# A two-layer PEER encoder: layer 0 also dense for 224 tokens in its V stage with a third sparse group, activations copied in pieces during U2, one-number gathers as steps of their own, x turned in 16 columns

## The chip, the cores and the metric

The kernel runs on one core of a Trainium2 chip. The metric is the device time of one execution in microseconds (us), the median over several runs. A profile is one execution that the hardware profiler recorded. Engines: PE is TensorE's matmul, PEld its weight load, DVE is VectorE, ACT is ScalarE, POOL is GpSimd, SP is SyncE, whose queue issues the plain loads.

## What is computed

A trunk of two layers for 256 tokens of width 1024, with 16 learned tokens put in front (272 tokens in layer 0, 256 in layer 1). Layer 0's mixer is a gated linear recurrence in both directions, layer 1's a conformer convolution. Each mixer is followed by PEER, which takes most of the time and all of the change:

```python
def peer_block(xc, w_query, sub_keys, expert_u, expert_v):
    ...
    s1, i1 = lax.top_k(scores[:, :, 0], PEER_TOPK)
    s2, i2 = lax.top_k(scores[:, :, 1], PEER_TOPK)
    cand = (s1[..., :, None] + s2[..., None, :]).reshape(c, PEER_HEADS, PEER_TOPK * PEER_TOPK)
    s, flat = lax.top_k(cand, PEER_TOPK)
    ...
    expert = idx1 * PEER_N_KEYS + idx2
    g = jax.nn.softmax(s.astype(jnp.float32), axis=-1).astype(xc.dtype)
    u = expert_u[expert]
    act = jax.nn.gelu(jnp.einsum('chkd,cd->chk', u, xc))
    v = expert_v[expert]
    return jnp.einsum('chk,chkd->cd', g * act, v)
```

Each token has 8 heads, each head picks 16 of 128 x 128 experts, and an expert is a row u and a row v of 1024 numbers.

## The kernel before

**Dense tokens.** Most tokens are computed against all 16,384 experts and the unpicked ones weighted with zero. Stage U loads the u rows as 128 pieces j of 128 rows (512 KB each). Each is split into a rounded part hi (ACT, L143) and a rest lo (DVE or POOL, L150), and 24 matmuls (L178) give the products of 128 experts with all dense tokens; ACT puts their gelu into `act_a` (j below 64, stage U1) or `act_b` (stage U2). In U2 the routing weights are made as products of one-hot matrices, 8 tokens to a unit (`g_unit`, L639 to L663), and multiplied into the activations of those tokens that are dense in V too. Stage V loads the v rows in the same way. For each j, eight matmuls of hi with the activations' two parts side by side (L701, twice as wide as the number of dense tokens) and eight of lo (L705, as wide as the number) add to eight accumulators that stay in PSUM. DVE makes the activations' second part for four j at a time (`w`, L262).

**Sparse groups.** The remaining tokens go in groups of 16; with 8 heads, a group fills the 128 partitions. A group of the early kind needs for each of its 16 picks one gathered u row per partition (L975, 512 KB a gather), a product with x (L984, "dot"), then one gathered v row (L975) and a multiply-add into `few_out` (L1024, "add"; the first is L1022). Ten of the early group's 16 dots run in U1 already. At the end eight pairs of matmuls (L740) put `few_out` on the accumulators. A late group does the same but picks its experts during V. A drawn group was dense in U: its picked activations already stand in `act_a` and `act_b`, so the whole activations of its 16 tokens are copied (POOL, L993), dumped as a table to DRAM (L995), and 16 gathers of one number per partition (L999, a "draw") fetch the picked ones; then come its v rows.

Which tokens are which is set by `DENSE_U`, `DENSE_V`, `EARLY`, `LATE` and `DRAWN` for (layer 0, layer 1). Before: layer 0 has 240 dense tokens, one early and one late group and no drawn one; layer 1 has 240 dense in U and 208 in V, one early and two drawn groups.

**Order.** `few_plan` lists the groups' steps one after the other, 70 in layer 0 and 72 in layer 1, and spreads them evenly over 111 of V's 128 j; `few_step`, called once per j, gives out what is due, one step of the pending picks (top-16 of scores on DVE: MAX, MAX_INDEX, MATCH_REPLACE, then softmax) included. The scheduler then orders every engine's queue, and each engine runs its queue strictly in that order. Row buffers: three, so a gather needs the add of three rows before. lo has two buffers, hi three, raw loads four. The x of a sparse group (`wide`) is made by matmuls of x with the unit matrix (`few_pick`), from copies of x's columns for the 8 heads that POOL writes (`xw`, L943), and is saved to DRAM and reloaded by `few_load` in V.

Of the kernel before, what the change touches and what calls it, by code (L numbers as in the profile page):

```python
# [31 lines left out]
CC = 8  # L32
HC = 8
FEW = META
DENSE_U, DENSE_V = (240, 240), (240, 208)
EARLY, LATE, DRAWN = ((256,), (240,)), ((240,), ()), ((), (224, 208))
DOTS_FROM, DOTS, AHEAD, LO_FROM = 48, 10, 2, 41
JG = 4
JA = 64
FULL = (("v", 1024),)  # L40
SQ_AT = 4
PE_TAPS = (0, 0, 0, 0, 0, 6, 31, 31)
# [18 lines left out]
class Trunk:  # L61
# [481 lines left out]
    def peer(self, layer, n, xs):  # L543
# [10 lines left out]
        with tc.tile_pool(name=f"few{layer}", bufs=1) as kp:  # L554
# [5 lines left out]
            with tc.tile_pool(name=f"top{layer}", bufs=1) as sp:  # L560
# [30 lines left out]
                drawn = [self.few_pick(sp, kp, q, xs, layer, t0) for t0 in DRAWN[layer]]  # L591

                def u_store(j, ps):
                    if j >= LO_FROM and len(picked[-1]) == 2:
                        with tc.issue_after(self.dve_lo.ins):
                            try:
                                next(slow)
                            except StopIteration as end:
                                picked[-1] += end.value
                    k, step = divmod(3 * (j - DOTS_FROM), 4)  # L600
                    if early and 0 <= k < DOTS + AHEAD and step < 3:
                        with tc.issue_after(self.dve_lo.ins), tc.issue_after(self.lo_ins.ins):
# [12 lines left out]
                    if 0 < t <= len(picked) and not odd:
                        with tc.issue_after(last.ins), tc.issue_after(self.mm.ins):
                            self.topk_out(*picked[t - 1], iT, ghT, glT)
                self.linears([U[j] for j in range(JA)], xs, nu, lambda j: FULL if j >= LO_FROM else (("p", 1024),), u_store)

            with tc.tile_pool(name=f"act1{layer}", bufs=1) as ap1:  # L620
                act_b = ap1.tile([P, NK - JA, nu], F32, name="act_b")
                hot_pool = tc.tile_pool(name=f"hot{layer}", bufs=2)
                hp = hot_pool.__enter__()

                def weigh(dst, g):
                    nc.vector.scalar_tensor_tensor(dst, g, scale, dst, op0=OP.mult, op1=OP.mult)  # L626
# [41 lines left out]
                def u_out(i, ps):  # L668
                    cd = at[0] * CC
                    w = act_b[:, i, :]  # L670
                    if cd < nu:
                        nc.scalar.activation(w[:, cd:], ps[:, cd:], AF.Gelu_apprx_tanh)
                    if cd > 0:
                        tmp = hp.tile([P, n], F32, tag="tmp", name="tmp")
                        nc.scalar.activation(tmp[:, :cd], ps[:, :cd], AF.Gelu_apprx_tanh)
                        nc.vector.tensor_tensor(w[:, :cd], w[:, :cd], tmp[:, :cd], op=OP.mult)  # L676
                    upto = min(len(chunks), (i + 1) * len(chunks) // (NK - JA - 4))
                    for c0 in chunks[at[0]:upto]:
                        g_unit(c0, JA + i + 1)
                    at[0] = upto  # L680

                acc = []
                self.upper(f"gate{layer}")
                self.linears([U[j] for j in range(JA, NK)], xs, nu, (("v", 1024),), u_out)
                hot_pool.__exit__(None, None, None)
                with tc.tile_pool(name=f"drawn{layer}", bufs=1) as sp:
                    for few in drawn:
                        self.few_dump(sp, few, act_a, act_b, layer)
                idx_pool.__exit__(None, None, None)
                self.upper(f"high{layer + 1}")  # L690
                row_pool = tc.tile_pool(name=f"rows{layer}", bufs=1)
# [228 lines left out]
    def few_pick(self, sp, kp, q, xs, layer, t0):  # L920
# [12 lines left out]
               "act": kp.tile([P, TOPK], F32, name=f"act{t0}"), "z": kp.tile([P, TOPK], F32, name=f"z{t0}")}  # L933
        if drawn:
            return few
        wide = sp.tile([P, D], F32, tag="kept" if early else "rows", name="wide", bufs=1 if early else AHEAD + 1)
        for h in range(2):
            pw = self.bank(5 + h, "wide_ps")
            for lo in range(2):
                xw = sp.tile([P, 4, HEADS, FEW], F32R, tag="xw", name="xw", bufs=2)  # L940
                for k in range(4):
                    src = xs(4 * h + k, lo).bitcast(F32)[:, None, t].to_broadcast([P, HEADS, FEW])
                    nc.gpsimd.tensor_copy(xw[:, k], src)  # L943
                for k in range(4):
                    nc.tensor.matmul(pw[:, k * P:(k + 1) * P], xw[:, k].rearrange("p h t -> p (h t)"), self.eye,
                                     start=k + lo == 0, stop=k + lo == 4, skip_group_check=True)
            nc.scalar.activation(wide[:, 512 * h:512 * h + 512], pw, AF.Copy)
        kept = self.dp.tile([P, D], F32, name=f"wide{layer}_{t0}")
        nc.sync.dma_start(kept, wide)
        return few | {"x": wide, "kept": kept}  # L950

    def few_topk(self, sp, few, layer):
        nc = self.nc
# [32 lines left out]
        if nxt < hi:  # L986
            few["rows"][nxt] = self.few_rows(pool, few, self.a["u_rows"], 0, nxt, ahead + 1)

    def few_dump(self, sp, few, act_a, act_b, layer):
        nc, t = self.nc, slice(few["t0"], few["t0"] + FEW)  # L990
        own = sp.tile([P, NK, FEW], F32, name=f"own{few['t0']}", bufs=1)
        for part, act in ((own[:, :JA], act_a), (own[:, JA:], act_b)):
            nc.gpsimd.tensor_copy(part, act[:, :, t])  # L993
        few["table"] = self.dp.tile([P, NK, FEW], F32, name=f"own{layer}_{few['t0']}")
        nc.gpsimd.dma_start(few["table"], own)  # L995

    def few_draw(self, few):
        for k in range(TOPK):
            self.nc.gpsimd.indirect_dma_start(  # L999
                out=few["act"][:, k:k + 1], out_offset=None, in_=few["table"].rearrange("p j (t o) -> (p j t) o", o=1),  # L1000
                in_offset=bass.IndirectOffsetOnAxis(ap=few["ids"][:, 0, k:k + 1], axis=0))

    def few_gelu(self, few, last):
        self.nc.scalar.activation(few["act"], few["act"], AF.Gelu_apprx_tanh)
        if last:
            self.warm(AF.Abs_reciprocal_sqrt)

    def few_load(self, vp, few):
        few["x"] = vp.tile([P, D], F32, tag="wide", name="wide", bufs=2)
        self.nc.sync.dma_start(few["x"], few["kept"])  # L1010

    def few_weigh(self, few, scale):
        self.nc.vector.scalar_tensor_tensor(few["act"], few["act"], scale, few["z"], op0=OP.mult, op1=OP.mult)
# [13 lines left out]

    def few_plan(self, vp, kp, early, late, drawn, scale, layer, ahead=2):
        steps = []
        for few in early + late + drawn:  # L1030
            lo = DOTS if few in early else 0
            if few["drawn"]:
                steps += [lambda few=few: self.few_draw(few)]
            else:
                steps += [lambda few=few: self.few_load(vp, few)]
                steps += [lambda few=few, lo=lo, k=k: self.few_dot(vp, few, k, lo, TOPK, ahead) for k in range(TOPK - lo + ahead)]
# [268 lines left out]
```

## Time and profile before

| | us |
|---|---|
| median of 3 runs | 1842.99 (1842.84 to 1844.76) |
| profiled execution | 1845.79 |
| its span | 1844.0 |
| layer 0: stage U1 / U2 / V, about | 176 to 345 / 345 to 556 / 556 to 890 |
| layer 1: mixer / U1 / U2 / V, about | 890 to 1051 / 1099 to 1272 / 1272 to 1472 / 1472 to 1816 |
| PE busy in the span | 1774.1 |

A row of a timeline gives start, duration, engine, line, operation and tiles (out<-in), and in brackets how long the engine had been idle before it and what ended that. A row of groups gives count, busy time, mean ns of one, idle time before. In windows the last three numbers are the granted TensorE clock (1.00 is full), the busy share of the 16 DMA engines, and GB/s.

### The profile page before, as it was taken

What the parts mean: (1) busy time and instruction counts of PE and PEld (TensorE: products, weight loads), DVE (VectorE), ACT (ScalarE), POOL (GpSimd) and SP (SyncE); (2) the same over time, 40 slices, a digit from 0 to 9 for tenths busy, and PEclk for the clock granted to TensorE, in tenths of its full rate; (3) what the DMA queues carried; (4) which work ended last, traced back from release to release, by engine and by line L of the source; (5) the groups of instructions that cost most, each with busy time, mean ns of one, the idle gap of its engine ahead of it and who ended that gap; (6) DMA issues with size and microseconds to landing.
All of it is one profiled execution on the core that took longest, in us unless ns stands there. A gap on an engine that the chain in (4) does not pass through costs nothing.

```text
span 1844.0 us, 35027 instructions
## 1 busy us (share of the span) xinstructions
PE 1774.1 (96%) x13500; PEld 1696.2 (92%) x13500; DVE 1513.8 (82%) x2863; ACT 916.2 (50%) x1510; POOL 486.1 (26%) x346
## 2 busy tenths in 40 slices
PE   8999999999999999999998999999999977999996
PEld 7899999999998999999887999999999967999996
DVE  7786996989999777786799869968889876868775
ACT  6544444454444545875432554445544534445552
POOL 1113993100002222130000129931000057423210
PEclk9999999999999999999999999999999988999998
DMA  5444567755558888887441445677555566889883
GB/s 195 160 161 145 185 196 247 247 169 164 162 173 305 289 306 278 294 318 238 161 140 35 140 154 185 196 250 246 171 171 171 173 251 226 311 304 341 293 293 126
DMA packets 111257, 395.17 MB, mean 214 GB/s; under 512 B 13169, under 2 KB 14321, under 8 KB 110705
## 3 DMA queue, kind: packets, MB, share of 16 engines
q1 hardware_dynamic: 91344, 323.69, 52.6%
q0 software_dynamic: 19744, 69.23, 10.5%
q8 instruction: 106, 1.74, 0.4%
q14 instruction: 63, 0.51, 0.1%
HBM read 385.99 MB, written 6.88 MB: 213 GB/s over the span
## 4 chain that ended last, share of the span: by engine, by line
PE 63%; DVE 8%; DMA 4%; issue 3%; POOL 2%; ACT 1%; POOLq 0%; DVEq 0%; ACTq 0%
PE u L178 30%; PE acc L701 18%; PE acc L705 10%; DVE cy L1185 2%; DMA rows<-peer_v,ids 2%; DVE odd L1185 2%; PE g L656 1%; PE g L657 1%; DVE lo L150 1%; DMA rows<-u_rows,ids 1%; POOL act L999 1%; POOL lo L150 1%; PE pre L234 0%; DMA raw<-peer_v 0%; PE sps L575 0%
## 5 line engine op out<-in xcount | busy, mean ns | idle before, releaser
L143 ACT ACTIVATE hi<-raw 128x1024 fp32r<-128x1024 f32 x556 | 588.7, 1060 | 649.6 <-PE u L178 227.6
L150 DVE TENSOR_TENSOR lo<-raw,hi 128x1024 fp32r<-128x1024 f32 x474 | 578.7, 1225 | 183.4 <-PE acc L705 70.4
L178 PE MATMUL u<-xs,hi 128*128 128x240 f32 (+2 forms) x4544 | 569.4, 277 | 0.6 <-DVE xs L377 0.6
L178 PEld LDWEIGHTS u<-xs,hi 128*128 128x128 f32 x4544 | 537.6, 189 | 1.4 <-DVE xs L377 1.0
L701 PE MATMUL acc<-w,hi 128*128 128x480 f32 (+1 forms) x1984 | 451.4, 370 | 3.1 <-DVE w L262 1.9
L701 PEld LDWEIGHTS acc<-w,hi 128*128 128x128 f32 x1984 | 358.2, 191 | 27.7 <-DVE w L262 2.3
L178 PE MATMUL u<-xs,lo 128*128 128x240 f32 (+2 forms) x2272 | 307.6, 276 | 6.7 <-POOL lo L150 3.6
L705 PEld LDWEIGHTS acc<-w,lo 128*128 128x128 f32 x2048 | 270.7, 192 | 39.7 <-DVE lo L150 31.9
L705 PE MATMUL acc<-w,lo 128*128 128x240 f32 (+1 forms) x2048 | 275.1, 276 | 27.8 <-DVE lo L150 27.8
L178 PEld LDWEIGHTS u<-xs,lo 128*128 128x128 f32 x2272 | 280.6, 189 | 8.2 <-POOL lo L150 4.3
L150 POOL TENSOR_TENSOR lo<-raw,hi 128x1024 fp32r<-128x1024 f32 x82 | 210.9, 2586 | 79.3 <-ACT hi L143 56.0
L975 POOL DMA_INDIRECT rows<-peer_v,ids x80 | 125.6, 1570 | 255.7 <-DVE few_out L1024 145.5
L975 POOL DMA_INDIRECT rows<-u_rows,ids x48 | 59.9, 1247 | 400.6 <-DVE sv L853 216.7
L214 PE MATMUL u<-x,raw 128*128 128x272 f32 x480 | 114.8, 399 | 5.2 <-DMA x<-h 5.2
L214 PEld LDWEIGHTS u<-x,raw 128*128 128x128 f32 x480 | 93.0, 194 | 24.8 <-DMA raw<-w_in 5.1
L1024 DVE SCALAR_TENSOR_TENSOR few_out<-rows,act,few_out 128x1024 f32<-128x1024 f32 x75 | 96.0, 1280 | 14.7 <-DMA rows<-peer_v,ids 14.6
L663 ACT ACTIVATE act_b<-g 128x432 f32<-128x432 f32 (+41 forms) x56 | 21.9, 390 | 108.5 <-DVE act_b L626 94.9
L639 DVE TENSOR_TENSOR AB<-iota,iT 128x2048 f16<-128x2048 f16 x56 | 68.1, 1219 | 0.1
L984 DVE SCALAR_TENSOR_TENSOR rows<-rows,wide 128x1024 f32<-128x1024 f32 x48 | 58.5, 1218 | 10.7 <-DMA rows<-u_rows,ids 10.7
L993 POOL COPY own<-act_a 128x1024 f32<-128x1024 f32 x2 | 3.9, 1970 | 211.4 <-DVE act_b L676 211.4
L656 PE MATMUL g<-AB 128*128 128x128 f16 x448 | 56.6, 220 | 0.0
L657 PE MATMUL g<-Bl,AB 128*128 128x128 f16 x448 | 56.0, 219 | 0.0
(280 smaller groups left out, 1818.9 us busy)
## 6 DMA issues: line engine op xcount, KB each, us to landing
raw<-peer_u SPq DMA_DIRECT2D x256, 512.0 KB, 4.1
raw<-peer_v SPq DMA_DIRECT2D x248, 512.0 KB, 4.8
raw<-w_query SPq DMA_DIRECT2D x28, 512.0 KB, 3.6
raw<-pw SPq DMA_DIRECT2D x22, 512.0 KB, 3.5
raw<-w_in SPq DMA_DIRECT2D x16, 512.0 KB, 3.9
raw<-w_out SPq DMA_DIRECT2D x8, 512.0 KB, 4.2
raw<-peer_v SPq DMA_DIRECT2D x16, 256.0 KB, 4.0
wide<-wide SPq DMA_DIRECT2D x6, 512.0 KB, 3.3
```

The lines of the kernel that those rows point to most:

```text
L143: self.act_hi = nc.scalar.activation(hi, raw, AF.Copy).ins
L150: i = e.tensor_tensor(lo[:, s], raw[:, s], hi[:, s].bitcast(F32), op=OP.subtract)
L178: self.mm = nc.tensor.matmul(ps[:, :n], l[:, k, :], xs(k, r)[:, :n], start=start, stop=stop)
L214: self.mm = self.nc.tensor.matmul(ps[:, :n], raw[:, k, :], x[:, k, :n], start=k == 0, stop=k == NB - 1)
L639: nc.vector.tensor_tensor(AB.rearrange("p x c (a b) -> p (x c) a b", b=2), keys, iT[:, c0 // HC].rearrange("p x c b -> p (x c) b")[:, :, N ...
L656: nc.tensor.matmul(ps[:, c, :], A, Bh, start=True, stop=False)
L657: nc.tensor.matmul(ps[:, c, :], A, Bl, start=False, stop=True)
L701: self.mm = nc.tensor.matmul(acc[b][:, :2 * n].rearrange("p (a t) -> p a t", a=2), hi, w[:, :, :n], start=j == 0, stop=j == NK - JG - 1, s ...
L705: self.mm = nc.tensor.matmul(main[b][:, :n], hi if p_ else lo, w[:, i, :n], start=False, stop=j == NK - 1 and not p_, skip_group_check=True)
L975: self.nc.gpsimd.indirect_dma_start(out=t, out_offset=None, in_=table, in_offset=bass.IndirectOffsetOnAxis(ap=few["ids"][:, i, k:k + 1], a ...
L1024: nc.vector.scalar_tensor_tensor(few["out"], t, w, few["out"], op0=OP.mult, op1=OP.add)
L1185: nc.vector.scalar_tensor_tensor(z, h, w, z, op0=OP.mult, op1=OP.add)
```

## The change

- In layer 0 V is dense for 224 tokens instead of 240, and tokens 224 to 239 become a third, drawn group.
- The activations of drawn groups are copied and dumped in pieces of 32 j (`few_dump`), each when its j are finished, instead of all together after U2. The last piece, j 96 to 127, is finished with U2's last matmul. The pieces have a pool of their own on the right side of SBUF, open during U2 only; the second pieces reuse its two buffers.
- A draw is a step for each of its 16 gathers, placed by the plan at j of its own, instead of one step of 16. Layer 0's plan now has 90 steps beside the draws, layer 1's 70.
- x of a sparse group is turned once, in 16 columns, and written to DRAM eight times over (a broadcast); it is loaded at j = 41 of U1 for the early group, and by `few_load` in V as before. POOL's copies `xw` are gone.

```diff
-DENSE_U, DENSE_V = (240, 240), (240, 208)
-EARLY, LATE, DRAWN = ((256,), (240,)), ((240,), ()), ((), (224, 208))
+DENSE_U, DENSE_V = (240, 240), (224, 208)
+EARLY, LATE, DRAWN = ((256,), (240,)), ((240,), ()), ((224,), (224, 208))
...
+JD = 32
...
+                    if j == LO_FROM:
+                        for few in early:
+                            self.few_load(sp, few, "kept", 1)
...
+                drawn_pool = tc.tile_pool(name=f"drawn{layer}", bufs=2, side="right")
+                rp = drawn_pool.__enter__()
+                dumps = {}
+                for g, few in enumerate(drawn):
+                    few["table"] = self.dp.tile([P, NK, FEW], F32, name=f"own{layer}_{few['t0']}")
+                    for j in range(0, NK, JD):
+                        dumps.setdefault(j + JD - 1 - JA if j >= JA else (g * JA + j) // JD * 8 + 3, []).append((few, j))
...
+                    for few, j in dumps.get(i, ()):
+                        few_dump(few, j)
...
+                def few_dump(few, j):
+                    own = rp.tile([P, JD, FEW], F32, tag="own", name="own")
+                    act, o = (act_a, j) if j < JA else (act_b, j - JA)
+                    nc.gpsimd.tensor_copy(own, act[:, o:o + JD, few["t0"]:few["t0"] + FEW])
+                    nc.gpsimd.dma_start(few["table"][:, j:j + JD], own)
...
-                with tc.tile_pool(name=f"drawn{layer}", bufs=1) as sp:
-                    for few in drawn:
-                        self.few_dump(sp, few, act_a, act_b, layer)
+                drawn_pool.__exit__(None, None, None)
...
-                xw = sp.tile([P, 4, HEADS, FEW], F32R, tag="xw", name="xw", bufs=2)
                 for k in range(4):
-                    src = xs(4 * h + k, lo).bitcast(F32)[:, None, t].to_broadcast([P, HEADS, FEW])
-                    nc.gpsimd.tensor_copy(xw[:, k], src)
...
-                    nc.tensor.matmul(pw[:, k * P:(k + 1) * P], xw[:, k].rearrange("p h t -> p (h t)"), self.eye,
+                    nc.tensor.matmul(pw[:, k * P:(k + 1) * P], xs(4 * h + k, lo)[:, t], self.eye,
...
             if few["drawn"]:
-                steps += [lambda few=few: self.few_draw(few)]
+                draws += [(len(steps), lambda few=few, k=k: self.few_draw(few, k)) for k in range(TOPK)]
...
+        first = 12 * (len(late) + 1)
+        for i, (at, f) in enumerate(draws):
+            g, k = divmod(i, TOPK)
+            lo, hi = first + 12 * g, self.steps[at][0] - 3
+            draws[i] = lo + k * (hi - lo) // TOPK, f
+        self.steps = sorted(self.steps + draws, key=lambda s: s[0])
```

Lines move by a little: L150 becomes L151, L262 L263, L975 L989, L999 L1004, L1022 L1027, L1024 L1029, L853 L870.

How the queues change, at three places. First POOL, from the end of layer 0's U1 through its V. `rows` are gathered rows, `ids_1815` belongs to the early group, `ids_2087` (after: `ids_2067`) to the late one. Before:

```order
L943 CAST xw<-xs_1065 128x128 x8
L943 CAST xw<-xs_1066 128x128 x8
L150 TENSOR_TENSOR lo<-raw,hi 128x1024 x39
L975 DMA rows<-u_rows,ids_1815 128x1024 x16
L975 DMA rows<-peer_v,ids_1815 128x1024 x16
L975 DMA rows<-u_rows,ids_2087 128x1024 x16
L975 DMA rows<-peer_v,ids_2087 128x1024 x16
```

And after the change, from the end of U2, with `ids_2102` for the drawn group and `own_224_4267` for its table:

```order
L698 COPY own<-act_b 128x512
L699 DMA own_224_4267<-own 128x512
L989 DMA rows<-u_rows,ids_1815 128x1024 x6
L989 DMA rows<-peer_v,ids_1815 128x1024 x3
L1004 DMA act_2103<-own_224_4267,ids_2102 128x1 x11
L989 DMA rows<-peer_v,ids_1815 128x1024
L1004 DMA act_2103<-own_224_4267,ids_2102 128x1 x5
L989 DMA rows<-peer_v,ids_1815 128x1024 x12
L989 DMA rows<-u_rows,ids_2067 128x1024 x16
L989 DMA rows<-peer_v,ids_2067 128x1024 x16
L989 DMA rows<-peer_v,ids_2102 128x1024 x16
```

The draws stand in two lumps of 11 and 5, around the early group's fourth v row. In layer 1, V begins so before the change:

```order
L975 DMA rows<-u_rows,ids_12719 128x1024 x5
L999 DMA act_12992<-own_224_18055,ids_12991 128x1 x6
L975 DMA rows<-u_rows,ids_12719 128x1024
L999 DMA act_12992<-own_224_18055,ids_12991 128x1 x10
L975 DMA rows<-peer_v,ids_12719 128x1024 x3
L999 DMA act_13004<-own_208_18060,ids_13003 128x1 x16
L975 DMA rows<-peer_v,ids_12719 128x1024 x13
```

And after it:

```order
L989 DMA rows<-u_rows,ids_12787 128x1024 x5
L1004 DMA act_13040<-own_224_15216,ids_13039 128x1 x6
L989 DMA rows<-u_rows,ids_12787 128x1024
L1004 DMA act_13040<-own_224_15216,ids_13039 128x1 x10
L989 DMA rows<-peer_v,ids_12787 128x1024 x3
L1004 DMA act_13052<-own_208_15217,ids_13051 128x1 x16
L989 DMA rows<-peer_v,ids_12787 128x1024 x13
```

There nothing moved: the same lumps at the same places. Next DVE at the start of layer 0's V, after the change, with what each row waits for (`DMASW` are gathers and dumps, from POOL's queue; `sc_2065` are the scores of the late group):

```order
L263 TENSOR_TENSOR w<-act_a,w 128x224 [waits Activation_49] x4
L151 TENSOR_TENSOR lo<-raw,hi 128x1024 [waits DMAHW0_49,DVE_49,PE_49]
L687 TENSOR_TENSOR act_b<-act_b,tmp 128x224 [waits Activation_49]
L263 TENSOR_TENSOR w<-act_a,w 128x4x224 [waits Activation_49]
L870 MAX sv<-sc_2065 128x8 [waits DMASW4_49,DMASW5_49,DMASW3_49,Pool_49]
L870 MAX sv<-sc_2065 128x8
```

The first MAX of the late pick now waits for POOL and its dumps; before it waited for nothing (`L853 MAX sv<-sc_2085 128x8`, partly ahead of V). The pick's tiles lie where the pieces lay. Last DVE around the early group's adds in layer 0, after the change, from the lo behind the third w on (the add in the second row is the third, that in the fourth row the fourth):

```order
L151 TENSOR_TENSOR lo<-raw,hi 128x1024
L1029 SCALAR_TENSOR_TENSOR few_out<-rows,act_1816,few_out 128x1024
L151 TENSOR_TENSOR lo<-raw,hi 128x1024
L1029 SCALAR_TENSOR_TENSOR few_out<-rows,act_1816,few_out 128x1024
L151 TENSOR_TENSOR lo<-raw,hi 128x1024
L1029 SCALAR_TENSOR_TENSOR few_out<-rows,act_1816,few_out 128x1024
L263 TENSOR_TENSOR w<-act_a,w 128x4x224
L151 TENSOR_TENSOR lo<-raw,hi 128x1024 x2
```

Here an add stands between any two lo; before the change the steps stood wider apart and came later.

More of the change, by code (lines that the diff above doesn't have):

```diff
@@ L935, in few_pick @@
             return few
-        wide = sp.tile([P, D], F32, tag="kept" if early else "rows", name="wide", bufs=1 if early else AHEAD + 1)
+        turned = sp.tile([FEW, D], F32, tag="turned", name="turned", bufs=1)
         for h in range(2):
-            pw = self.bank(5 + h, "wide_ps")
+            pw = self.bank(5 + h, "wide_ps")[:FEW]
             for lo in range(2):
-                xw = sp.tile([P, 4, HEADS, FEW], F32R, tag="xw", name="xw", bufs=2)
                 for k in range(4):
-                    src = xs(4 * h + k, lo).bitcast(F32)[:, None, t].to_broadcast([P, HEADS, FEW])
-                    nc.gpsimd.tensor_copy(xw[:, k], src)
-                for k in range(4):
-                    nc.tensor.matmul(pw[:, k * P:(k + 1) * P], xw[:, k].rearrange("p h t -> p (h t)"), self.eye,
+                    nc.tensor.matmul(pw[:, k * P:(k + 1) * P], xs(4 * h + k, lo)[:, t], self.eye,
                                      start=k + lo == 0, stop=k + lo == 4, skip_group_check=True)
[L947 to L950, printed above, removed]
+            nc.scalar.activation(turned[:, 512 * h:512 * h + 512], pw, AF.Copy)
+        kept = self.dp.tile([HEADS, FEW, D], F32, name=f"wide{layer}_{t0}")
+        nc.sync.dma_start(kept.rearrange("h t d -> t h d"), turned[:, None, :].to_broadcast([FEW, HEADS, D]))
+        few["kept"] = kept
+        return few
     def few_topk(self, sp, few, layer):
@@ L987, in few_dot, with few_draw @@
             few["rows"][nxt] = self.few_rows(pool, few, self.a["u_rows"], 0, nxt, ahead + 1)
[L989 to L1001, printed above, removed]
+    def few_draw(self, few, k):
+        self.nc.gpsimd.indirect_dma_start(
+            out=few["act"][:, k:k + 1], out_offset=None, in_=few["table"].rearrange("p j (t o) -> (p j t) o", o=1),
+            in_offset=bass.IndirectOffsetOnAxis(ap=few["ids"][:, 0, k:k + 1], axis=0))
     def few_gelu(self, few, last):
@@ L1006, in few_gelu, with few_load @@
             self.warm(AF.Abs_reciprocal_sqrt)
-    def few_load(self, vp, few):
-        few["x"] = vp.tile([P, D], F32, tag="wide", name="wide", bufs=2)
-        self.nc.sync.dma_start(few["x"], few["kept"])
+    def few_load(self, pool, few, tag="wide", bufs=2):
+        few["x"] = pool.tile([P, D], F32, tag=tag, name="wide", bufs=bufs)
+        self.nc.sync.dma_start(few["x"], few["kept"].rearrange("h t d -> (h t) d"))
     def few_weigh(self, few, scale):
@@ L1029, in few_plan @@
         steps = []
+        draws = []
         for few in early + late + drawn:
```

## The prediction

> **What bounds the kernel now.** I read the busy shares and the chain of waits first.
>
> ```profile
> PE 1774.1 (96%) x13500; PEld 1696.2 (92%) x13500; DVE 1513.8 (82%) x2863; ACT 916.2 (50%) x1510; POOL 486.1 (26%) x346
> ...
> PE 63%; DVE 8%; DMA 4%; issue 3%; POOL 2%; ACT 1%; POOLq 0%; DVEq 0%; ACTq 0%
> ```
>
> TensorE bounds the whole, with 70 us idle. The windows by stage show where the two V stages differ: 556 to 890 is layer 0's, 1492 to 1816 most of layer 1's (columns: length, busy time of PE, PEld, DVE, ACT, POOL, granted clock, DMA share, GB/s).
>
> ```profile
> 345.00:556.00 211.00, 208.83 (x2083) 207.47 (x2081) 193.75 (x290) 101.99 (x224) 0.00 (x0) 1.00 0.55 171
> 556.00:890.00 334.00, 333.18 (x2028) 302.80 (x2029) 257.52 (x285) 199.30 (x298) 80.31 (x64) 1.00 0.83 291
> 1492.00:1816.00 324.00, 297.73 (x1940) 292.92 (x1940) 244.28 (x276) 150.89 (x154) 123.08 (x85) 0.96 0.82 288
> 556.00:606.00 50.00, 49.18 (x294) 44.37 (x295) 43.77 (x82) 24.91 (x31) 13.49 (x9) 1.00 0.83 295
> ```
>
> Layer 0's V stage is as long as its matmuls: 0.8 us idle of 334. Layer 1's already has the form that the change gives to layer 0 (a third group, and draws), and TensorE idles 26 us in it. Its timeline shows where.
>
> ```profile
> 1484.78 1.56 PE L705 MATMUL acc<-w,lo 128*128 128x208 f32 x8 [2.01 <-DVE lo L150]
> ...
> 1501.37 2.04 PE L705 MATMUL acc<-w,lo 128*128 128x208 f32 x8 [7.55 <-DVE lo L150]
> ...
> 1568.53 2.04 PE L705 MATMUL acc<-w,lo 128*128 128x208 f32 x8 [11.60 <-DVE lo L150]
> 1570.36 3.02 PE L701 MATMUL acc<-w,hi 128*128 128x416 f32 x8
> ```
>
> Behind the 11.60 stands DVE, which waited for a gathered row; behind that, POOL, which issued sixteen one-number gathers of the second drawn group ahead of the row. A dump of 2 MB stands behind the 7.55.
>
> ```profile
> 1565.12 1.28 DVE L1024 SCALAR_TENSOR_TENSOR few_out<-rows,act,few_out 128x1024 f32<-128x1024 f32 x1 [13.09 <-DMA rows<-peer_v,ids]
> ```
>
> ```profile
> 1482.86 0.54 POOL L995 DMA_DIRECT2D own<-own  x1 [0.30 <-POOL own L993]
> 1490.73 1.00 POOL L975 DMA_INDIRECT rows<-u_rows,ids  x1 [7.33 <-DMA own<-own]
> ...
> 1537.41 1.94 POOL L999 DMA_INDIRECT act<-own,ids  x1 [0.30 <-DVE z L971]
> ...
> 1541.04 0.94 POOL L999 DMA_INDIRECT act<-own,ids  x1 [0.30 <-issue]
> ...
> 1560.65 0.94 POOL L975 DMA_INDIRECT rows<-peer_v,ids  x1 [0.30 <-issue]
> ```
>
> A draw thus holds POOL for (1560.65 - 1537.41) / 16 = 1.45 us. The order of the queues, above, shows that the draws are spread in the source alone: in POOL's queue layer 1's 16 + 16 stand where they stood, and layer 0's new ones stand as 11 ahead of the fourth v row and 5 ahead of the fifth.
>
> **The narrower V stage of layer 0.** One j is two runs of eight matmuls, read from start to start.
>
> ```profile
> 704.29 1.92 PE L701 MATMUL acc<-w,hi 128*128 128x480 f32 x8
> ...
> 706.95 1.25 PE L701 MATMUL acc<-w,hi 128*128 128x480 f32 x5
> ```
>
> ```profile
> 1713.91 1.87 PE L740 MATMUL acc<-same,few_out 128*128 128x16 f32 x16
> 1715.63 1.76 PE L701 MATMUL acc<-w,hi 128*128 128x416 f32 x8
> 1717.23 1.04 PE L705 MATMUL acc<-w,lo 128*128 128x208 f32 x8
> 1718.11 1.69 PE L701 MATMUL acc<-w,hi 128*128 128x416 f32 x8
> ...
> 1720.51 1.68 PE L701 MATMUL acc<-w,hi 128*128 128x416 f32 x8
> ```
>
> Width 240 takes 2.66 us (706.95 - 704.29), 2.645 over many j; width 208 takes 2.40 (1720.51 - 1718.11). Sixteen tokens less are half of the difference, 0.12 us; over 124 j that is **-14.9**. The third group's sum matmuls cost 1.72 (1715.63 - 1713.91): **+1.7**. Two routing units fewer in stage U2 save about a microsecond each by the row below, with whose runs those of L657 interleave (30.3 us over 30 units): **-2.0**.
>
> ```profile
> L656 PE MATMUL g<-AB 128*128 128x128 f16 x240 | 30.3, 220 | 0.0
> ```
>
> **What layer 0's V stage gains in waits.** Let t run from 556.35, where DVE begins the first w; these are DVE's rows there.
>
> ```profile
> 556.35 1.37 DVE L262 TENSOR_TENSOR w<-act_a,w 128x240 fp32r<-128x240 f32 x4
> ...
> 559.09 0.29 DVE L853 MAX8 sv<-sc 128x8 f32<-128x128 f32 x1
> ...
> 565.44 1.21 DVE L150 TENSOR_TENSOR lo<-raw,hi 128x1024 fp32r<-128x1024 f32 x1
> ...
> 579.24 0.17 DVE L963 TENSOR_TENSOR ids<-row,idx 128x16 uint32<-128x16 f32 x1
> ...
> 583.15 0.17 DVE L971 COPY z<-z 128x16 f32<-128x16 f32 x1
> ```
>
> Here are the landing times of that stage's 256 KB loads and v rows, and the old dumps' copies:
>
> ```profile
> raw<-peer_v SPq DMA_DIRECT2D x8, 256.0 KB, 3.9
> rows<-peer_v,ids POOLq DMA_INDIRECT x29, 6.9
> ```
>
> ```profile
> L993 POOL COPY own<-act_b x2: 1032/1044/1056, 1477.9 to 1481.5; 128x1024 f32<-128x1024 f32 x2
> ```
>
> *The dump.* The pick's first MAX, in order ahead of a lo, now waits until the last dump has landed. The page shows no 256 KB dump; its nearest rows are the 0.54 issue above and a 256 KB load, 3.9 to landing. With a copy of 0.8 (the row's 1.04 is for twice as much; beside DVE it may take more than half), begun at about t = 1, it lands at 1 + 0.8 + 0.3 + 0.54 + 3.9, so t = 6.6 where MAX stood at 2.7: DVE is 3.9 late, and half a microsecond more goes to the dot behind it. Before, the lo for j = 3 ended at 566.65, and TensorE, which reached it at 556.35 + 2.3 + 3 x 2.645 = 566.6, has nothing to spare. **+4.5** (0, if the landing is as short as the copy, to +6). The Trainium skill ("DMA: Bandwidth & Descriptors", section "Anatomy of one DMA — SWDGE (gpsimd) path") gives 2.0 us and bytes over 436 GB/s, an estimate of 2.6 us for 256 KB; by it the sum would be 1.3 less. No run shows such a dump yet.
>
> *DVE's load.* In the first 50 us DVE was busy 43.77. A second pick and 90 steps instead of 70 add to it. What one costs, I read from DVE's groups between MAX and z, 559.09 to 583.3.
>
> ```profile
> L150 DVE TENSOR_TENSOR lo<-raw,hi 128x1024 fp32r<-128x1024 f32 x8 | 9.7, 1217 | 0.0
> L984 DVE SCALAR_TENSOR_TENSOR rows<-rows,wide 128x1024 f32<-128x1024 f32 x3 | 3.7, 1219 | 0.0
> L262 DVE TENSOR_TENSOR w<-act_a,w 128x960 fp32r<-128x960 f32 x3 | 3.5, 1152 | 0.4 <-ACT w L259 0.4
> ```
>
> Without these, 24.2 - 9.7 - 3.7 - 3.5 leaves 7 us for a pick whose first half of MAX steps ran ahead of V. With those steps, which V now holds for both picks, I count 9.5 more. 18 j of steps hold 14.6 instead of 11.4, 3.2 x 1.2 = 3.9 more. That is 43.8 + 13.4 = 57 in 50, so **+6** (0 to +8).
>
> *The draws.* A pick took 559.09 to 583.15, 24.1 us, with its indices 20.2 in. Two back to back, 3.9 late, put the draws' indices at 2.7 + 3.9 + 24.1 + 20.2 = 50.9. Then 11 draws of 1.45 keep the fourth v row from POOL until 67, and 6.9 later it lands, t = 74. On DVE its add (1.28) stands ahead of a lo (1.22), the one for j = 21, which is ready at 76.4. TensorE needs it at 2.3 + 21 x 2.53 = 55.5, and 66 with the two delays above: **+10**. Five more draws put the fifth row's issue at 75.5, its landing at 82.4, and the next lo, behind an add and a w, at 86, against 79: **+7**. Nothing covers this: lo has two buffers, so TensorE is at most two j behind DVE.
>
> *The clock.* After 7.55 idle the eight L705 matmuls took 2.04 instead of 1.04, and after 11.60 L701 3.02 instead of 1.69 too: 1.0 to 2.3 for an idle time. Two of them: **+3**. By the Trainium skill ("TensorE: Matmul & The Clock Gate", "Part 1: The HAM clock gate") the clock halves after an idle window of about 3.4 us. Here eight matmuls took 1.56 already after 2.01 idle, so on smaller gaps the trace differs; by the page as by the rows, both new stalls are long enough.
>
> *Denser steps.* 90 steps in 111 j are one per 1.23 j, 3.12 us, each a row of 512 KB: 168 GB/s; V's own loads are 512 KB in 2.53 us, 207. Together 375 GB/s. Layer 1, at the busiest, shows this:
>
> ```profile
> 1740.00:1770.00 30.00, 30.00 (x200) 29.87 (x199) 26.65 (x24) 14.93 (x15) 13.22 (x8) 1.00 0.96 354
> ```
>
> If 354 is the most there is, 60 gathers at 3.12 take 6% longer, +11; the pauses of about five steps between groups give half of it back: **+5** (0 to +11). The Trainium skill, in that DMA page's section "Where 436 GB/s comes from", has about 358 GB/s from HBM for a core and 435 for the fabric. The trace's 354 at a share of 0.96 agrees with the first; by the second this term would be 0.
>
> Stage sum: -14.9 + 1.7 + 4.5 + 6 + 10 + 7 + 3 + 5 = +22.3 (+5 to +37).
>
> **Layer 1.** The same dump arrives earlier here. It was issued at 1482.86 and its last byte was waited for until 1490.73. The new last pieces are a quarter each: two copies (1.6), two issues (1.4), 3.9 to landing, from 1476 on: 1483. The row gathers gain 7, but MAX waits too, and the pick behind it; I take **-5** for the draws and all behind them (-2 to -7). The fourth add stands one lo later in DVE's queue than before, so TensorE does one j (2.40) more ahead of the long wait, **-2.4**, and half a microsecond of slow clock. The clump of 16 draws itself stays, and so does the 11.60. Sum **-8** (-4 to -11).
>
> **Edits that cost nothing.** The first dump of each layer, in U1, stands among POOL's lo:
>
> ```profile
> 243.56 2.40 POOL L150 TENSOR_TENSOR lo<-raw,hi 128x1024 fp32r<-128x1024 f32 x1 [0.29 <-ACT hi L143]
> 246.25 2.41 POOL L150 TENSOR_TENSOR lo<-raw,hi 128x1024 fp32r<-128x1024 f32 x1 [0.29 <-PE u L178]
> ```
>
> They have 2.69 a j (246.25 - 243.56) and take 2.40, and POOL waits for TensorE to free a buffer, so its lead covers most of the dump's 2 us (0 to +1). Those in U2 find POOL idle (0.00 busy in 211). Turning x in 16 columns removes casts that TensorE never waited for; its matmuls keep their count. The reloaded x is needed seven j, 19 us, after its load.
>
> **Sum.** 22.3 - 2.0 - 8 = +12.3 on the profiled execution's own 1845.8 (span 1844.0), so 1858.1. That run lies 2.8 above the median of the three, 1843.0, so the forecast is **1855**. Less than 0.2%, 3.7 us, cannot be told from no change.
>
> **Rivals.** *Faster (0.20).* DVE has the room that I deny it and the dump lands unnoticed, so that the indices are ready when the seventeenth lo is, at 2.3 + 16.5 x 2.53 = 44; the draws take 0.94 + 0.30 as the shortest did. Then the fourth row is issued at 57.6, its lo is ready at 67 against 55.5, and the second at 75 against 58: 17 us of wait, not 27.5. With the clock at +2, no price for the denser steps, layer 1 at -11: -14.9 + 1.7 + 17 + 2 - 2 - 11 = -7, **1836**. It decides at the indices: ready by t = 45, faster. Against it is the 43.77 of 50.
>
> *No change (0.14).* Half of that: V at about +12, so 12 - 2 - 8 = +2, **1845**. For it speaks that DVE's room in the second half of those 50 us was larger than in the first.
>
> *Much slower (0.14).* The gathers' round trip sets the pace of the adds. A row in layer 1 takes this long to land when the DMA engines are this full:
>
> ```profile
> rows<-peer_v,ids POOLq DMA_INDIRECT x41, 8.4
> ```
>
> ```profile
> 620.87 0.94 POOL L975 DMA_INDIRECT rows<-peer_v,ids  x1 [0.65 <-DVE few_out L1024]
> ```
>
> With an add (1.28) and 0.65 of handing over, three buffers return in 10.3 us, 3.44 a row against a step of 3.12: 60 x 0.32 = +19 where I put 5: **1869**.
>
> *The spreading isn't there.* That is in the forecast: queue order, not source order, decides.
>
> **How the numbers follow.** The forecast has 0.52, wholly slower. Slower is 0.52 + 0.14 = 0.66, same 0.14, faster 0.20. The range reaches from just inside the faster case, 1834, to a little over the much slower one, 1872.
>
> **What would show it.** Right: matmuls of width 448 and 224 at 2.53 a j; in V of layer 0 two idle times on TensorE, behind lo, of 7 to 10 us within 90 us from its start, with DVE waiting for v rows and POOL in draws; the first MAX waiting for the dump; layer 1's long wait still there and earlier. Wrong: layer 0's V with under 15 us idle, draws under 1.2 us, or the indices before t = 45. If the stalls are there and the time is not longer, the error is in layer 1's term.

## The result, and the profile after

The changed kernel takes 1862.5 us (median of 4 runs, 1861.5 to 1869.6) against 1843.5 for the kernel before (4 runs): **19 us slower**, a ratio of 1.0091 with a 95% interval of 1.0072 to 1.0109. The profiled execution's span is 1860.9 instead of 1844.0, 16.9 more.

A second profile of the changed kernel (below, `again`) has the same span, 1860.8, and complete records in the place that matters, so I read the waits there. First the table of stages. A stage runs from its first matmul to that of the next; "end" is what follows the first matmul that transposes the output.

| | to U1 | U1, U2 | V, layer 0 | to V of layer 1 | V, layer 1 | end | span |
|---|---|---|---|---|---|---|---|
| before | 176.6 | 380.2 | 344.1 | 572.8 | 346.9 | 23.4 | 1844.0 |
| after | 172.3 | 380.7 | 370.9 | 571.7 | 338.6 | 26.8 | 1860.9 |
| after, `again` | 173.4 | 378.6 | 369.2 | 574.5 | 338.2 | 26.8 | 1860.8 |

Layer 0's V lost 25 to 27 us. Layer 1's V gained 8.3 to 8.7. The start gained 3 to 4, and the end lost 3.4. The windows of the changed kernel (`again`; all rows of this section are from there) show what layer 0's V now looks like, as a whole and in the 40 us after its first 48 (columns as above).

```profile
552.00:921.00 369.00, 337.78 (x2111) 315.61 (x2111) 290.27 (x378) 200.38 (x305) 125.66 (x98) 0.97 0.83 290
600.00:640.00 40.00, 27.00 (x153) 25.10 (x152) 23.32 (x33) 11.88 (x13) 25.10 (x23) 0.83 0.63 216
```

Before, TensorE idled 0.8 of 334; now 31 of 369, and 13 of these lie in 40 us, at a granted clock of 0.83. POOL is busy 25 of the 40. Its timeline there:

```profile
586.49 0.94 POOL L989 DMA_INDIRECT rows<-peer_v,ids  x1 [4.89 <-DVE rows L998]
600.59 0.95 POOL L1004 DMA_INDIRECT act<-own,ids  x1 [13.16 <-DVE ids L973]
601.84 1.48 POOL L1004 DMA_INDIRECT act<-own,ids  x1 [0.30 <-issue]
...
614.62 0.94 POOL L1004 DMA_INDIRECT act<-own,ids  x1 [0.30 <-issue]
615.87 0.94 POOL L989 DMA_INDIRECT rows<-peer_v,ids  x1 [0.30 <-issue]
617.11 0.94 POOL L1004 DMA_INDIRECT act<-own,ids  x1 [0.30 <-DMA act<-own,ids]
...
622.63 0.94 POOL L1004 DMA_INDIRECT act<-own,ids  x1 [0.30 <-issue]
623.87 0.94 POOL L989 DMA_INDIRECT rows<-peer_v,ids  x1 [0.30 <-issue]
```

Eleven draws take POOL from 600.59 to 615.87 before it issues the early group's fourth v row, and five more keep the fifth until 623.87. DVE waits for both rows, and a lo stands behind each add (behind the last one shown, after a w):

```profile
609.67 1.28 DVE L1029 SCALAR_TENSOR_TENSOR few_out<-rows,act,few_out 128x1024 f32<-128x1024 f32 x1
610.87 1.26 DVE L151 TENSOR_TENSOR lo<-raw,hi 128x1024 fp32r<-128x1024 f32 x1
620.22 1.28 DVE L1029 SCALAR_TENSOR_TENSOR few_out<-rows,act,few_out 128x1024 f32<-128x1024 f32 x1 [8.09 <-DMA rows<-peer_v,ids]
621.42 1.22 DVE L151 TENSOR_TENSOR lo<-raw,hi 128x1024 fp32r<-128x1024 f32 x1
629.04 1.28 DVE L1029 SCALAR_TENSOR_TENSOR few_out<-rows,act,few_out 128x1024 f32<-128x1024 f32 x1 [6.39 <-DMA rows<-peer_v,ids]
```

And TensorE waits for lo, twice, and runs slowly after each wait (1.05 and 1.78 are the usual times of the two groups):

```profile
584.77 1.99 PE L722 MATMUL acc<-w,lo 128*128 128x224 f32 x8 [2.06 <-DVE lo L151]
...
610.11 1.05 PE L722 MATMUL acc<-w,lo 128*128 128x224 f32 x8
610.99 1.78 PE L718 MATMUL acc<-w,hi 128*128 128x448 f32 x8
612.61 1.05 PE L722 MATMUL acc<-w,lo 128*128 128x224 f32 x8
613.50 1.78 PE L718 MATMUL acc<-w,hi 128*128 128x448 f32 x8
622.70 2.05 PE L722 MATMUL acc<-w,lo 128*128 128x224 f32 x8 [7.42 <-DVE lo L151]
624.54 2.39 PE L718 MATMUL acc<-w,hi 128*128 128x448 f32 x8
632.52 2.05 PE L722 MATMUL acc<-w,lo 128*128 128x224 f32 x8 [5.58 <-DVE lo L151]
634.37 2.58 PE L718 MATMUL acc<-w,hi 128*128 128x448 f32 x8
```

The narrower stage itself is there: 2.51 a j (613.50 - 610.99) where it was 2.66 (706.95 - 704.29 in the prediction).

### The profile page after: what moved, and what is told of

It is laid out like the page before. It is cut to its first block, busy times and chain, and to the rows that moved or that the text cites. A ratio compares the mean times of both kernels' runs of the same rounds, so it can differ in the third digit from the quotient of the medians.

```text
span 1860.9 us, 35089 instructions
## 1 busy us (share of the span) xinstructions
PE 1765.7 (95%) x13488; PEld 1694.7 (91%) x13488; DVE 1524.4 (82%) x2915; ACT 913.4 (49%) x1515; POOL 524.7 (28%) x348
## 4 chain that ended last, share of the span: by engine, by line
PE 72%; DVE 12%; DMA 5%; issue 5%; POOL 3%; ACT 2%; another core or an unknown queue 0%; POOLq 0%; DVEq 0%; SPq 0%; ACTq 0%
PE u L179 41%; PE acc L718 14%; PE acc L722 9%; PE u L215 2%; DMA raw<-peer_v 2%; DVE lo L151 2%; DMA rows<-peer_v,ids 2%; DVE cy L1197 2%; DVE odd L1197 2%; POOL lo L151 1%; PE g L667 1%; POOL rows L989 1%; PE g L668 1%; PE sps L576 1%; ACT hi L144 1%
## 5 line engine op out<-in xcount | busy, mean ns | idle before, releaser
L151 DVE TENSOR_TENSOR lo<-raw,hi 128x1024 fp32r<-128x1024 f32 x474 | 578.5, 1225 | 177.0 <-PE u L179 76.5
L718 PE MATMUL acc<-w,hi 128*128 128x448 f32 (+1 forms) x1984 | 442.2, 365 | 5.5 <-issue 2.8
L718 PEld LDWEIGHTS acc<-w,hi 128*128 128x128 f32 x1984 | 361.8, 193 | 19.9 <-issue 3.5
L722 PE MATMUL acc<-w,lo 128*128 128x224 f32 (+1 forms) x2048 | 276.9, 277 | 45.7 <-DVE lo L151 35.1
L151 POOL TENSOR_TENSOR lo<-raw,hi 128x1024 fp32r<-128x1024 f32 x82 | 211.3, 2595 | 105.9 <-ACT hi L144 83.1
L989 POOL DMA_INDIRECT rows<-peer_v,ids x96 | 150.7, 1570 | 243.8 <-DVE few_out L1029 137.3
L1029 DVE SCALAR_TENSOR_TENSOR few_out<-rows,act,few_out 128x1024 f32<-128x1024 f32 x90 | 115.3, 1281 | 20.0 <-DMA rows<-peer_v,ids 19.9
L698 POOL COPY own<-act_b 128x512 f32<-128x512 f32 x6 | 6.4, 1086 | 386.5 <-ACT act_b L683 386.5
L989 POOL DMA_INDIRECT rows<-u_rows,ids x48 | 61.9, 1290 | 161.8 <-DVE rows L998 128.9
L674 ACT ACTIVATE act_b<-g 128x488 f32<-128x488 f32 (+39 forms) x54 | 21.0, 388 | 104.9 <-DVE act_b L637 93.6
L1004 POOL DMA_INDIRECT act<-own,ids x48 | 53.2, 1108 | 32.1 <-DVE ids L973 18.1
```

Source lines behind the costliest of these rows:

```text
L151: i = e.tensor_tensor(lo[:, s], raw[:, s], hi[:, s].bitcast(F32), op=OP.subtract)
L718: self.mm = nc.tensor.matmul(acc[b][:, :2 * n].rearrange("p (a t) -> p a t", a=2), hi, w[:, :, :n], start=j == 0, stop=j == NK - JG - 1, s ...
L722: self.mm = nc.tensor.matmul(main[b][:, :n], hi if p_ else lo, w[:, i, :n], start=False, stop=j == NK - 1 and not p_, skip_group_check=True)
L989: self.nc.gpsimd.indirect_dma_start(out=t, out_offset=None, in_=table, in_offset=bass.IndirectOffsetOnAxis(ap=few["ids"][:, i, k:k + 1], a ...
L1004: self.nc.gpsimd.indirect_dma_start(out=few["act"][:, k:k + 1], out_offset=None, in_=few["table"].rearrange("p j (t o) -> (p j t) o", o=1) ...
L1029: nc.vector.scalar_tensor_tensor(few["out"], t, w, few["out"], op0=OP.mult, op1=OP.add)
```

## The experiments

**The same kernel again.**

> The changed kernel once more, to see which of its waits come back. Theory (the draws stand in a lump ahead of the early group's v rows in POOL's queue): V of layer 0 again idles TensorE 7 to 10 us at the fourth and fifth v row, about 70 us from its start. In the first profile DVE and ACT also stood still for 8 us there (622 to 630) with nothing that the trace names as their releaser. If that belongs to the lump it comes back at the same place; if it is an accident of one execution it is gone, and the span is some 5 us shorter. Expected 1862 (1860 to 1866).

It took 1862.6. The two waits came, 7.4 and 5.6, as rows above show. The 8 us in which DVE and ACT stood still without a named releaser in the first profile did not come back; there the two waits show as one of 9.4 with other idle time around it, and the spans are equal. So that gap says nothing of the kernel.

**Layer 0's tokens put back.** One line, the rest of the change stays:

```diff
-DENSE_U, DENSE_V = (240, 240), (224, 208)
-EARLY, LATE, DRAWN = ((256,), (240,)), ((240,), ()), ((224,), (224, 208))
+DENSE_U, DENSE_V = (240, 240), (240, 208)
+EARLY, LATE, DRAWN = ((256,), (240,)), ((240,), ()), ((), (224, 208))
```

> Only layer 0's tokens are put back (240 dense in V, no drawn group there); dumps in pieces, draws as steps and x in 16 columns stay. Theory: what is left is layer 1's gain, -8 on the kernel before, so 1835 (1832 to 1839). Rival (layer 1 gains nothing by itself and the -8 in the trace is the DMA or clock state that layer 0's change left behind): 1843 (1841 to 1845).

1832.3 (1831.8 to 1836.0), 0.9942 of the kernel before (0.9923 to 0.9961). V of layer 0 is back at 344.1, V of layer 1 is at 338.0, and U1 begins at 172.8. The theory holds, at the lower edge of its range, and 3.8 us more come from a place where I had put nothing: U1 begins earlier. There the matmuls that turn x stand, before the change and here (the stages around them are the same):

```profile
166.79 3.04 PE L945 MATMUL wide_ps<-eye,xw 128*128 128x128 f32 x16
173.72 3.04 PE L945 MATMUL wide_ps<-eye,xw 128*128 128x128 f32 x16
```

```profile
166.73 1.20 PE L958 MATMUL wide_ps<-eye,xs 128*16 128x128 f32 x16
171.81 1.20 PE L958 MATMUL wide_ps<-eye,xs 128*16 128x128 f32 x16
```

Sixteen take 1.20 instead of 3.04, twice in layer 0. And V of layer 1 still has its long wait, which is 10.3 here instead of 11.6; the first one is 6.8 instead of 7.6 plus 2.0:

```profile
1484.61 2.04 PE L722 MATMUL acc<-w,lo 128*128 128x208 f32 x8 [6.76 <-DVE lo L151]
...
1559.59 2.04 PE L722 MATMUL acc<-w,lo 128*128 128x208 f32 x8 [10.34 <-DVE lo L151]
```

**Layer 0's draws left out.**

```diff
     def few_draw(self, few, k):
+        if len(DRAWN[0]) and few["layer"] == 0:
+            if k == 0:
+                self.nc.gpsimd.memset(few["act"], 0.0)
+            return
```

> Layer 0's sixteen draws are left out (that group's activations are set to zero instead), all else as changed. Theory: the lump holds up the early group's fourth and fifth v row and costs 15 to 20 with the slow clock behind it, so 1845 (1840 to 1850). Rival (DVE's load, the dump and the denser gathers make the wait, and the draws only stand beside it): over 1856.

A further line, not shown, tells a group its layer. The drawn group's activations are zero here, so the result is not the reference's. 1843.1 (10 runs, 1835.0 to 1854.6, the widest spread of all kernels here): 19.4 less than with them. V of layer 0 takes 356.1, and no wait in it is longer than 2.2 us. So 13 of the 25 us that layer 0's V lost (369.2 - 356.1) go with the lump, about half. The profiled executions differ by 17.6, and the other 4 lie in stages that have no draw of layer 0: 1.4 ahead of U1, 1.5 between the V stages, 1.3 at the end. The rest of V's loss is still there: 356 is 12 more than before the change, for matmuls that need some 15 less.

**The draws truly spread.** A memset on DVE of the column that a draw fills makes the draw wait for DVE to come to that j, so the order is one that POOL's queue keeps (lines move by one):

```diff
     def few_draw(self, few, k):
+        self.nc.vector.memset(few["act"][:, k:k + 1], 0.0)
```

> Each draw is tied to a memset of its own column on DVE, behind the lo of the j that the plan gives it, so that POOL's queue spreads the draws in both layers: between v rows, never more than four in a row. Theory: layer 0 loses the lump (-15 to -18), layer 1 its two (some -8 to -12, of the 13 us that TensorE idles there): 1837 (1831 to 1845). Rival (DVE's load and the gathers' round trip set the pace): over 1856 in layer 0's part, 1852 to 1858 in all.

1832.7 (1830.1 to 1835.3), ratio 0.9943 (0.9922 to 0.9964); a second time 1833.2, ratio 0.9937 (0.9914 to 0.9961). Thirty us less than the changed kernel from 48 memsets. POOL now issues the fourth v row 12 us earlier and layer 0's draws one or two at a time between rows, the first at 625:

```profile
603.70 0.94 POOL L989 DMA_INDIRECT rows<-peer_v,ids  x1 [16.06 <-DVE ids L977]
...
625.40 0.95 POOL L1005 DMA_INDIRECT act<-own,ids  x1 [0.30 <-issue]
...
634.05 0.95 POOL L1005 DMA_INDIRECT act<-own,ids  x1 [0.30 <-issue]
```

V of layer 0 takes 350.7, V of layer 1 326.4 (338.6 with the lumps, 346.9 before). No wait over 2.4 is left in layer 0's V (2.9 in the second profile), and in layer 1's the long one of 10 us is gone; its first, of 4.8, is not.

Layer 0's V is 5.4 shorter so than without any draw. TensorE idles as long in both (19.1 and 19.9); it is busy for less time, 331.6 against 336.2. Why its matmuls were slower without the draws is not shown, so between the two runs the lump's price in this stage lies at 13 to 19 us.

> The spread draws of both layers once more, on one chip with the next kernel. 1833 (1830 to 1837).

**Both parts together.**

> Both earlier edits together: layer 0's tokens put back, and layer 1's draws spread by memsets on DVE. Theory: the parts add up. V of layer 1 took 338.0 with its lumps and 326.4 with the draws spread, so 1832.3 - 11.6 = 1821 (1818 to 1824), the fastest of all so far. Rival (part of the spread kernel's short layer 1 comes from elsewhere): 1826 or more.

1824.4 (1822.5 to 1827.9), ratio 0.9886 (0.9867 to 0.9905), 3 above what the sum gave; V of layer 1 took 330.2. It was run once more beside the spread kernel:

> Layer 0's tokens put back and layer 1's draws spread, once more, on one chip with the kernel before it. If parts add up, it is 11 to 12 faster than layer 0's tokens put back alone (1832.3), so 1821; the first time it came out at 1824.4. Either way below the spread kernel by 8 to 12: 1822 (1819 to 1826).

1822.6 (1821.5 to 1825.7), ratio 0.9879 (0.9863 to 0.9896), against the 1833.2 of the spread kernel beside it. V takes 344.1 and 327.3. The parts add up within 2 to 3 us, and of the kernels that compute the whole result this is the fastest: **the change without its new tokens in layer 0, and with draws that are spread in the queue and not in the source alone.**

**Half the bytes.** Layer 0's V with the draws spread is still 6.6 longer than before the change. To see whether the landing rows cost that, each gathered row is made half as wide, and DVE's work kept by lines not shown that use the half twice (so the result is not the reference's):

```diff
-            out=t, out_offset=None, in_=table,
+            out=t[:, :512], out_offset=None, in_=table.rearrange("r (b d) -> (r b) d", b=2),
```

> Draws spread, and every gathered u or v row is 512 wide instead of 1024 (half the bytes; the DVE work is kept at full size by using the half twice, so the sparse groups' results are not the reference's). Theory (landing rows at 334 to 350 GB/s are what is late in the denser steps, the prediction's +5): the waits behind landing rows, 8 us in layer 0's V after its first 90 us and some 6 in layer 1's, go: 1821 (1816 to 1826). Rival (DVE's queue itself is what is late): 1830 to 1834.

1815.5 (1813.6 to 1817.1), ratio 0.9840 (0.9820 to 0.9860), a little more of a gain than the theory's range allowed. Layer 0's V falls from 350.7 to 340.9. The windows from 640 to 860, first with full rows (spread), then with half rows:

```profile
640.00:860.00 220.00, 212.21 (x1351) 200.33 (x1350) 180.39 (x190) 140.95 (x231) 95.57 (x64) 1.00 0.90 323
```

```profile
640.00:860.00 220.00, 220.00 (x1411) 209.23 (x1411) 187.55 (x227) 144.15 (x234) 99.61 (x64) 1.00 0.80 268
```

TensorE's 7.8 us of idle go to nothing with DVE busier than before, so it was not DVE's queue. What DVE waited for with full rows was landing rows, 9.7 us in 7 waits (second row, 640 to 870), and with half rows that line is missing:

```profile
DVE w L263 <- ACT w L260: 13.2, 13, 2.8
DVE few_out L1030 <- DMA rows<-peer_v,ids: 9.7, 7, 1.8
```

Whether the rows land sooner because they are smaller or because the DMA engines are less full (share 0.80 instead of 0.90) this run can't tell; both are bytes.

**The pick later.** Two edits were to price the first 80 us of V, where with the draws spread TensorE has these waits:

```profile
560.51 1.16 PE L722 MATMUL acc<-w,lo 128*128 128x224 f32 x8 [1.57 <-DVE lo L151]
564.60 1.15 PE L722 MATMUL acc<-w,lo 128*128 128x224 f32 x8 [1.31 <-DVE lo L151]
584.98 2.05 PE L722 MATMUL acc<-w,lo 128*128 128x224 f32 x8 [2.22 <-DVE lo L151]
592.69 1.15 PE L722 MATMUL acc<-w,lo 128*128 128x224 f32 x8 [0.95 <-DVE lo L151]
630.66 1.15 PE L722 MATMUL acc<-w,lo 128*128 128x224 f32 x8 [2.29 <-DVE lo L151]
```

One begins the drawn group's pick at j = 30 (and its draws at j = 42, not shown), the other both picks at j = 3:

```diff
-            while self.picks:
+            while self.picks and (j >= 30 or self.layer or len(self.picks) > 1):
```

```diff
-            while self.picks:
+            while self.picks and (j >= 3 or self.layer):
```

> Draws spread, and in layer 0 the drawn group's pick starts at j = 30 instead of right behind the late group's, its draws from j = 42. Theory (a second pick in the first 50 us overloads DVE, the prediction's +6): the waits of 2.2, 1.0 and 2.3 within 80 us of V's start go, so 1828 (1825 to 1830) against the 1832.7 of the spread draws alone. Rival (DVE had the room, these waits are landing rows): 1831 to 1835.

> Draws spread, and layer 0's picks begin at j = 3 instead of 0, so that no lo stands behind a MAX that waits for the dump. Theory (the dump's wait, the prediction's +4.5): the two first waits of V, 1.6 and 1.3, go: 1830 (1828 to 1831.5). Rival (the dot behind the late gather, or DVE's total load, brings them back): 1832 to 1834.

Neither gained: 1837.4 (10 runs, 1833.1 to 1841.5; ratio 0.9958, 0.9946 to 0.9969) and 1839.0 (7 runs; 0.9964, 0.9948 to 0.9979), both at or a little above the spread kernel, whose intervals they overlap. In the first, the waits at 592 and 630 are gone as expected, and others stand where the pick now is:

```profile
638.59 1.15 PE L722 MATMUL acc<-w,lo 128*128 128x224 f32 x8 [1.93 <-DVE lo L151]
...
646.19 1.15 PE L722 MATMUL acc<-w,lo 128*128 128x224 f32 x8 [0.70 <-DVE lo L151]
649.86 1.15 PE L722 MATMUL acc<-w,lo 128*128 128x224 f32 x8 [0.91 <-DVE lo L151]
715.30 2.05 PE L722 MATMUL acc<-w,lo 128*128 128x224 f32 x8 [2.95 <-DVE lo L151]
```

In the second, 1.6 and 1.3 became 2.2 and 1.4 a few j later, and V grew to 356.8. There MAX no longer waits for the dump; ahead of the first of these waits DVE stands before a dot whose u row has not landed:

```profile
566.64 1.23 DVE L998 SCALAR_TENSOR_TENSOR rows<-rows,wide 128x1024 f32<-128x1024 f32 x1 [3.53 <-DMA rows<-u_rows,ids]
```

My theory that the first 50 us were a place of overload, with room behind, falls: the second pick cost TensorE about 3 us in both places (0.95 + 2.29, and 1.93 + 0.70 + 0.91). And what the wait for the dump costs by itself is not shown, since without it another wait took its place. Giving the dumps memory that the pick doesn't use was not tried.

**Each draw twice.**

```diff
-        self.nc.gpsimd.indirect_dma_start(
-            out=few["act"][:, k:k + 1], ...
+        for act in ("act", "twin")[:2 if few["layer"] == 0 else 1]:
+            self.nc.gpsimd.indirect_dma_start(
+                out=few[act][:, k:k + 1], ...
```

> The changed kernel with each of layer 0's draws issued twice, the second into a tile that nothing reads; they stand next to each other in the same two lumps. Theory: a draw in the lump costs what it holds POOL, 1.25 to 1.45 us, so 16 more add 20 to 23 to layer 0's V: 1883 (1878 to 1888). And the time behind the last output transfer, which rose from 4.6 to 8.0 us as POOL's count of DMAs rose from 162 to 204, rises by another 1.3 for 16 more. Rival (the lump's cost is the landing of the draws or the order of the rows, not the issue): 1862 to 1870, and no longer end.

1867.1 (2 runs, 1863.3 and 1870.8), 4.5 more: in the rival's range, though two runs so far apart don't resolve 4.5. Layer 0's V took 380.0, 9 to 11 more and not 20. POOL did issue for that much longer, with the last draw at 647.14 instead of 622.63:

```profile
613.77 0.94 POOL L1005 DMA_INDIRECT act<-own,ids  x1 [0.30 <-issue]
615.02 0.94 POOL L989 DMA_INDIRECT rows<-peer_v,ids  x1 [0.30 <-issue]
...
625.49 0.94 POOL L989 DMA_INDIRECT rows<-peer_v,ids  x1 [0.30 <-issue]
...
635.56 0.94 POOL L989 DMA_INDIRECT rows<-peer_v,ids  x1 [0.30 <-issue]
...
647.14 0.94 POOL L1005 DMA_INDIRECT twin<-own,ids  x1 [0.30 <-issue]
```

But the scheduler now put rows between (after 11, 7, 6, 6 and 2 draws), so the draws don't stand in the same two lumps, and each row landed while the next draws were issued. DVE's ninth add came 13.9 later (656.29 against 642.40). So the price followed how late the rows came, and not the sum of the issue times. The end became shorter (21.6 against 26.8), so my guess that POOL's count of DMAs lengthens it was wrong.

## Why the prediction was right, and where it was off

It said slower, 1855 (1834 to 1872), for lumps of draws in layer 0's V. The mechanism is shown: without the lump 19 us go, and with the draws spread, in both layers, 30.

- *The narrower stage:* -14.9 said; 2.505 a j over many j instead of 2.645 is -17.4 over 124 j. I had taken half of the difference between widths 240 and 208; the steady rate at 224 is below the middle. Sum matmuls +1.7 said, +1.9 measured (3.7 to 5.6 busy).
- *The draws:* the indices at t = 50.9 said, 48.5 measured (600.14); 1.45 a draw said, 1.39 measured; the fourth row issued at t = 67 said, 64.3 measured. Its add began 4.4 later (620.22), not 6.9, in a stretch where the DMA engines' share was 0.63. So the waits were 7.4 and 5.6 where I said 10 and 7. The row to take was the landing time in a quiet stretch, which the stall itself makes.
- *The clock:* +3 said. PE's busy time in this stage is 338.0; 341.6 before, less 17.4, plus 1.9, would be 326.1. So 11.9 are left over for slow matmuls. Of this, 6.5 is gone with the draws spread (331.6). **This is the term that was sized most wrongly:** I had counted only the two long waits, and the short ones slow TensorE too. After a wait of 2.06 the next eight took 1.99 instead of 1.05. Summed over the trace, matmuls that took over 1.3 times their usual time make up 9.3 of the 11.9: 4.0 behind the two long waits, 3.5 behind those of 2.06 and 2.52.
- *The dump and DVE's load:* +4.5 and +6 said; the four waits of the first 48 us come to 5.7 (1.50, 1.32, 2.06, 0.80). The dump landed 3.4 after its issue began (553.69 to 557.1), where I had 0.54 + 3.9. The Trainium skill's estimate ("DMA: Bandwidth & Descriptors", section "Anatomy of one DMA — SWDGE (gpsimd) path") was 2.6, less than the trace shows. The two later experiments moved these waits and removed none for good, so they don't tell the two terms apart.
- *Denser steps:* +5 (0 to +11) said; 9.8 shown by the half rows. If the 11 was right, the pauses between groups give nearly nothing back.
- *Layer 1:* -8 said, -8.3 and -8.7 (`again`) measured, by the mechanism named: the gather behind the dumps is issued 8.9 after V's first matmul where it was 17.0, the waits of 2.01 and 7.55 became one of 4.8, and the long wait went from 11.6 to 9.5, since the lump stays.
- *Nothing for the turned x:* this step failed. "Its matmuls keep their count" was true and beside the point: they got faster, 3.04 to 1.20 for sixteen, -3.7 in layer 0 and -1.8 of the matmuls' time in layer 1. The weight load went from 190 ns to 95 (below). The Trainium skill has a rule for this in "TensorE: Matmul & The Clock Gate", section "LDWEIGHTS (loading the stationary operand)": the time goes with the columns, 0.83 ns each, an estimate of 107 ns for 128 and 13 for 16. The rows agree in the direction and not in the size. I had not looked up the rule for the one matmul whose shape changed.
- *Two routing units fewer:* -2 said; U1 and U2 together went from 380.2 to 380.7 and 378.6, so it isn't resolved.
- *The end:* 3.4 longer, behind the last output transfer, and not foreseen. It is the same in both profiles of each kernel that has two and differs between kernels (21.6 to 26.8). Its cause stays open.

With the stage's idle time, 28.7 more than before, layer 0's V adds up: -17.4 + 1.9 + 28.7 + 11.9 = 25.1, the difference between 369.2 and 344.1 (it must, since the 11.9 are what is left over). Of the 28.7, 5.7 are the first four waits, 13.0 the two long ones, and 10.0 all others. That 25.1 comes so near to the 22.3 of the forecast is in part luck: the narrower matmuls, the first waits and the draws were 2.5, 4.8 and 4.0 below what I said, the clock and the remaining waits 8.9 and 5.0 above. The spans' difference, +16.9 where +12.3 was said, comes out of the steps: V of layer 0 4.5 more, the routing units 2.5, the end 3.4, and to the other side the start 4.3, the stretch between the V stages 1.1 and layer 1 0.3. The rest of the 7.5 by which the median was missed is the profiled execution's place: 2.8 above its median before, 0.2 after.

## What to carry to other kernels

Draws that were spread in the source stood in lumps on the chip until something held each of them at its place; so read the queue, not the source. Many small operations in a queue cost what waits behind them in it: here sixteen gathers of one number cost 13 to 19 us of the stage, about what it gained by its narrower matmuls, and a memset apiece on DVE took that price away. This stage had no idle time left, and work moved into it was paid for: the bytes of the gathered rows with up to 9.8 us, a second pick with about 3 at both places that were tried.

## What the runs showed of the hardware that was not expected

The weight loads of the matmuls that turn x, before and after the change (min/median/max in ns; 128 and 16 columns):

```profile
L945 PEld LDWEIGHTS wide_ps<-eye,xw x48: 186/190/192, 166.8 to 1093.0; 128*128 128x128 f32 x48
L945 PE MATMUL wide_ps<-eye,xw x48: 272/316/332, 166.8 to 1093.0; 128*128 128x128 f32 x48
```

```profile
L958 PEld LDWEIGHTS wide_ps<-eye,xs x48: 93/95/100, 165.7 to 1113.6; 128*16 128x16 f32 x48
L958 PE MATMUL wide_ps<-eye,xs x48: 218/223/305, 165.8 to 1113.7; 128*16 128x128 f32 x48
```

An eighth of the columns halves the load, and the matmuls follow each other in 75 ns (1.20 / 16) instead of 190. Short waits slow TensorE as long ones do, but not each time: after 2.06 (above) the next eight matmuls took 1.99, and in the kernel without layer 0's draws, after a longer wait, 1.15, near the usual time:

```profile
583.27 1.15 PE L722 MATMUL acc<-w,lo 128*128 128x224 f32 x8 [2.22 <-DVE lo L151]
```

What sets this is not shown.

A gathered row of 512 KB landed in 4.4 us (615.87 to 620.22 above) in a quiet stretch; the stage's median is 7.8.
